# Eight modulation columns held to program order on VectorE, in a one-core encoder layer

## The chip, the cores and the metric

The kernel runs on one core of a Trainium2 chip. The metric is the device time of one execution in microseconds, lower is better; the median of several runs is compared. The core has five engines that work side by side, each with a queue of its own that it takes in order: TensorE (PE) for matmuls, VectorE (DVE), ScalarE (ACT), GpSimd (POOL) and SyncE (SP), which here only issues DMAs.

## The reference

One encoder layer on 512 tokens of width 1024, in float32, with nine modulation vectors computed from a conditioning vector `c`:

```python
c_act = jax.nn.silu(c)
mod = c_act @ w_mod + b_mod                 # 9 vectors of 1024
(sh1, sc1, g1, sh2, sc2, g2, sh3, sc3, g3) = jnp.split(mod, 9, axis=-1)

h = modulate(rmsnorm(x, norm_ffn1), sh1, sc1)
x = x + 0.5 * g1 * swiglu(h, w_ffn1_in, w_ffn1_out)

h = modulate(rmsnorm(x, norm_mix), sh2, sc2)
qa, ka, va, qb, kb, vb, ga, gb = jnp.split(h @ w_in, SPLIT_POINTS, axis=-1)
ya = window_gqa_sink(rope(qa), rope(ka), va, sink) @ w_branch_a   # 8 heads, |i-j| <= 128
yb = diff_attention(rope(qb), rope(kb), vb, lam) @ w_branch_b     # 4 heads, each normalised
x = x + g2 * ((sigmoid(ga) * ya + sigmoid(gb) * yb) @ w_out)

h = modulate(rmsnorm(x, norm_ffn2), sh3, sc3)
x = x + 0.5 * g3 * swiglu(h, w_ffn2_in, w_ffn2_out)
```

## The kernel before

Activations lie transposed, features on the 128 partitions and the 512 tokens along the free dimension, so `x` is eight tiles of 128 x 512. Every float32 product is made of three matmuls of a high and a low part (`mm3`); `split_from` makes the parts: ScalarE casts the high one (L179), VectorE subtracts for the low one (L180). The core does one stage after another: first feed-forward, shared projections, differential attention beside the gates, window attention beside the last gates and the two branches, output product, second feed-forward.

**The modulation columns.** Each of the nine vectors is stored as eight columns of 128 values. `mod_col(v, c)` computes one: VectorE multiplies a 128 x 1024 tile of `w_mod` with the conditioning row, copied to all partitions, and sums along the row (L266, one instruction). The tile is loaded by `mod_load` (L237) on SP's queue, 512 KB. The first two vectors are made at the start; the other 56 columns are spread over the layer in three lists: `rest` (G1, SC2, SH2) beside the first feed-forward, `later` (G2, SC3, SH3) beside the projections, and `latest`, the eight of G3, beside the gates that are left when the differential attention has ended (L1517). `column(columns)` takes the next column of a list, issues its load and puts it on `asked`; when more than `COLUMNS[...]` are asked for (2 for `later` and `latest`), the oldest is summed. So the sum of a column is traced two loads behind its own load. `beside` calls `column` after every fourth step of a gate; the `while` behind it (L1518) sums what is left. G3 is used only where the second feed-forward's product is added to `x` (L1625).

**What sets the order.** The Python program is traced once, which gives every instruction a place in the program's order. In this part of the layer (L1501 to L1539) the order of window attention, gates and branches in the program comes from `Line`, a planner by hand with costs and due times. Then the scheduler of the framework orders each engine's queue: by its own cost model it takes the instruction that is ready, and of several the first in the program. Inside `manual_schedule` blocks the order of the named engines is the program's; the stretch of this change is in none. So an instruction whose inputs the scheduler takes for ready early can go far ahead of its place. `tc.keep_in_program_order(ins)` adds one edge, without a wait: `ins` may not be queued ahead of the one instruction that was traced just before it on its engine. What is traced after it is free to go ahead of it.

In the program G3's columns stand so: column 0 is traced directly behind the two small VectorE instructions that `mod_begin` makes on the first use of G3 (L256, they read only `par`), which follow the third of four `turn_queries_a`; column 1 behind the fourth; column 2 behind `window_scores` of the second unit (its last VectorE instruction is L1420); column 3 behind two `window_turn` splits; columns 4 and 5 behind the scores of the third and fourth unit; columns 6 and 7 behind the split of the first window block's output.

**Buffers.** The loads of G3's columns take tiles of the `u4` ring, which has six. The window attention's `mask`, the reloaded conditioning row (`cact[0]`) and the transposed probabilities of `window_turn` come from the same ring.

Neighbours that the steps below name: `diff_norm` normalises a head of the differential attention (L1250 transposes, L1258 sums of squares on ScalarE, L1259 to L1261 on VectorE, L1262 a power on GpSimd, L1263 and L1264 on VectorE), and `diff_end` transposes the result again (`turned`, L1111) and splits it (L1275, L1276). `start_a` reads the window queries and values back from DRAM (L1345 to L1348), `turn_queries_a` transposes them (L1111) and splits them. `then_a` (L1523) and `then_b` (L1531, L1533) take the branches' results.

Of the kernel before, what the change touches and what calls it, by code (L numbers as in the profile page):

```python
# [128 lines left out]
def layer(ctx: ExitStack, tc: tile.TileContext, a: dict):  # L129
# [104 lines left out]
    def mod_load(v, c, w=None):  # L234
        if w is None:
            w = u4(F32).rearrange("p a b -> p (a b)")
        nc.sync.dma_start(w, a["w_mod"][v * NC + c])  # L237
        return w
# [4 lines left out]
    def mod_begin(v):  # L243
        if v in (SH1, SH2, SH3):
            return par[:, BMOD + v * NC : BMOD + (v + 1) * NC]
        if v not in begins:
            n = len(begins) * NC
            t = begins[v] = begin[:, n : n + NC]
            b = par[:, BMOD + v * NC : BMOD + (v + 1) * NC]
            if v in norms:  # L250
                V.scalar_tensor_tensor(t, b, 1.0, par[:, norms[v] : norms[v] + NC], ALU.add, ALU.mult)
            elif v == G3:

                t, b = (u.rearrange("p (n j) -> p n j", n=2) for u in (t, b))
                for j, by in ((slice(0, 2), -0.5), (slice(2, 4), 0.5)):
                    V.tensor_scalar(t[:, :, j], b[:, :, j], by, None, ALU.mult)  # L256
            else:
                V.tensor_scalar(t, b, 0.5, None, ALU.mult)
        return begins[v]

    def mod_col(v, c, w=None, in_order=False):
        if w is None:
            w = mod_load(v, c)
        t, b = modv[v][:, c : c + 1], mod_begin(v)[:, c : c + 1]
        by = 1.0 if v in norms or v in (SH1, SH2, SH3) else -0.5 if v == G3 and c % 4 < 2 else 0.5
        ins = V.tensor_tensor_reduce(  # L266
            out=w, in0=w, in1=cact[0], scale=by, scalar=0.0 if v in norms else b, op0=ALU.mult, op1=ALU.add,
            accum_out=t,
        )
        if in_order:  # L270
            tc.keep_in_program_order(ins)
        if v in norms:
            V.scalar_tensor_tensor(t, t, par[:, norms[v] + c : norms[v] + c + 1], b, ALU.mult, ALU.add)
# [168 lines left out]
    class Unit:  # L442
# [13 lines left out]
        asked, length = ("s1", "a11", "a12", "a22"), 1.0  # L456
# [229 lines left out]
    rest = [(v, c) for v in (G1, SC2, SH2, G2, SC3, SH3, G3) for c in range(NC)]  # L686
    rest, later, latest = rest[: EARLY * NC], rest[EARLY * NC : (EARLY + NEXT) * NC], rest[(EARLY + NEXT) * NC :]
# [59 lines left out]
    class Out1:  # L747
# [38 lines left out]
        def after(self, m):  # L786
            while any((v, c) == (G1, m) for v, c, *_ in rest + asked):
                column(rest)
            V.scalar_tensor_tensor(x[m], self.bank[m], modv[G1][:, m : m + 1], x[m], ALU.mult, ALU.add)
            if self.final:  # L790
                n2.add(m)
                spill(m)
# [6 lines left out]
    credit, asked = [0.0], []  # L799
# [4 lines left out]
    def column(columns):  # L804

        if columns:
            v, c = columns.pop(0)
            asked.append((v, c, mod_load(v, c, room[len(columns) % 2] if columns is rest else None)))
        if asked and (len(asked) > COLUMNS[columns is rest] or not columns):
            mod_col(*asked.pop(0), in_order=columns is rest)  # L810

    def side1(n=SIDE):

        while small_loads and len(rest) < 20:
            nc.sync.dma_start(*small_loads.pop())
        credit[0] += n
        while (rest or asked) and credit[0] >= 1.0:
            credit[0] -= 1.0
            column(rest)

    with tc.manual_schedule(engines={mybir.EngineType.SP, mybir.EngineType.Pool}):
# [62 lines left out]
        while rest or asked:  # L884
            column(rest)
# [751 lines left out]
    class Plain(Unit):  # L1637
        asked, more = ("a11", "a12", "a21", "a22"), {}
# [261 lines left out]
```

## Time and profile before

| | us |
|---|---|
| median of 3 runs | 1076.38 |
| lowest, highest | 1075.57, 1079.63 |
| profiled execution, its own time | 1076.98 |
| its span, first to last instruction | 1075.2 |
| TensorE busy | 1050.4 |
| VectorE busy | 797.0 |
| ScalarE busy | 568.0 |
| GpSimd busy | 154.0 |

TensorE's granted clock is 0.999 in the mean. In rows of the timeline the columns are start, duration, engine, source line, operation, output<-inputs, shape, count, and in brackets the engine's idle time before it and what ended it; `SPq` is a queue's issue of a DMA. In rows of waits they are who waited, for whom, the sum in us, how often, and the longest. In rows of DMA issues the last number is the median time from issue to landing. In rows of groups they are count, busy time and mean ns, and idle time before.

### The profile page before, as it was taken

The page shows a single profiled execution, that of the slowest core. Times are in us where ns is not written, and L with a number is a line of the kernel's source. Part 1 is how long each engine was busy: PE and PEld are TensorE (multiplying, and loading weights), DVE is VectorE, ACT ScalarE, POOL GpSimd, SP SyncE. Part 2 cuts the span into 40 slices and gives each one's busy share as a digit, 9 for nine tenths or more (in the row PEclk, how much of TensorE's full clock was granted, in tenths as well). Part 3 has the DMA queues.
Part 4 walks back from the last instruction along what each step waited for, and adds up shares of the span by engine and source line. Part 5 has one row for each costly group of instructions (what it writes and reads, how often), then busy time and mean ns, then how long its engine had stood idle before and what let it go on. Part 6 is the DMA issues. An engine that isn't in the chain of part 4 may idle for free. (4 is left out here: it accounts for less than half of the span.)

```text
span 1075.2 us, 18690 instructions
## 1 busy us (share of the span) xinstructions
PE 1050.4 (98%) x7316; PEld 955.6 (89%) x7316; DVE 797.0 (74%) x1459; ACT 568.0 (53%) x928; POOL 154.0 (14%) x174
## 2 busy tenths in 40 slices
PE   8999999999999999999998999999899999999998
PEld 6689889899998988898777888989889999999998
DVE  6985667576796679858774688945779777877877
ACT  5564335244354442657775666524766546664553
POOL 1100010100110100442211101001011111211210
PEclk9999999999999999999999999999999999999999
DMA  9968788866885369696368943843398899998974
GB/s 327 361 212 198 208 213 250 213 177 183 255 201 160 130 234 411 209 252 166 84 159 255 262 165 107 291 120 83 94 244 193 211 234 234 201 229 202 216 151 123
DMA packets 69083, 220.92 MB, mean 205 GB/s; under 512 B 8193, under 2 KB 10881, under 8 KB 68994
## 3 DMA queue, kind: packets, MB, share of 16 engines
q1 hardware_dynamic: 46512, 146.52, 38.3%
q0 software_dynamic: 19488, 68.70, 34.7%
q10 hardware_dynamic: 2994, 4.51, 1.1%
q8 instruction: 57, 0.93, 0.3%
q14 instruction: 32, 0.26, 0.1%
HBM read 209.46 MB, written 10.23 MB: 204 GB/s over the span
## 5 line engine op out<-in xcount | busy, mean ns | idle before, releaser
L179 ACT CAST high<-raw 128x1024 fp32r<-128x1024 f32 (+2 forms) x162 | 159.1, 986 | 190.1 <-PE sc L169 43.6
L180 DVE TENSOR_TENSOR low<-raw,high 128x1024 fp32r<-128x1024 f32 (+2 forms) x162 | 184.2, 1141 | 62.2 <-ACT high L179 60.4
L438 PE MATMUL acc<-b,high 128*128 128x256 f32 x508 | 141.0, 278 | 0.8 <-ACT f L512 0.7
L439 PE MATMUL acc<-b,high 128*128 128x256 f32 x508 | 140.7, 277 | 0.2 <-DVE b L1695 0.2
L440 PE MATMUL acc<-b,low 128*128 128x256 f32 x508 | 140.5, 277 | 0.0
L438 PE MATMUL sc<-b,high 128*128 128x256 f32 x500 | 138.6, 277 | 0.3 <-DVE f L514 0.3
L440 PE MATMUL sc<-b,low 128*128 128x256 f32 x500 | 138.5, 277 | 0.0
L439 PE MATMUL sc<-b,high 128*128 128x256 f32 x500 | 138.5, 277 | 0.0
L179 ACT CAST high<-u 128x1024 fp32r<-128x1024 f32 (+1 forms) x74 | 76.6, 1034 | 89.3 <-PE sc L169 30.3
L180 DVE TENSOR_TENSOR low<-u,high 128x1024 fp32r<-128x1024 f32 (+1 forms) x74 | 88.9, 1201 | 30.9 <-ACT high L179 29.2
L168 PE MATMUL sc<-b,high 128*128 128x512 f32 (+1 forms) x280 | 101.2, 361 | 0.6 <-ACT b L179 0.6
L169 PE MATMUL sc<-b,high 128*128 128x512 f32 (+1 forms) x280 | 100.7, 360 | 0.2 <-DVE b L180 0.2
L170 PE MATMUL sc<-b,low 128*128 128x512 f32 (+1 forms) x280 | 100.5, 359 | 0.0
L438 PEld LDWEIGHTS acc<-b,high 128*128 128x128 f32 x508 | 95.4, 188 | 1.3 <-ACT f L512 0.9
L439 PEld LDWEIGHTS acc<-b,high 128*128 128x128 f32 x508 | 95.5, 188 | 0.5 <-DVE b L1695 0.4
L440 PEld LDWEIGHTS acc<-b,low 128*128 128x128 f32 x508 | 95.3, 188 | 0.1
L438 PEld LDWEIGHTS sc<-b,high 128*128 128x128 f32 x500 | 94.1, 188 | 0.7 <-DVE f L514 0.5
L440 PEld LDWEIGHTS sc<-b,low 128*128 128x128 f32 x500 | 93.9, 188 | 0.1
L439 PEld LDWEIGHTS sc<-b,high 128*128 128x128 f32 x500 | 93.9, 188 | 0.0
L168 PE MATMUL acc<-b,high 128*128 128x512 f32 (+1 forms) x248 | 92.8, 374 | 0.0
L170 PE MATMUL acc<-b,low 128*128 128x512 f32 (+1 forms) x248 | 90.2, 364 | 0.0
L169 PE MATMUL acc<-b,high 128*128 128x512 f32 (+1 forms) x248 | 90.1, 363 | 0.0
(368 smaller groups left out, 2678.1 us busy)
## 6 DMA issues: line engine op xcount, KB each, us to landing
u<-w_mod SPq DMA_DIRECT2D x48, 512.0 KB, 7.5
raw<-w2i SPq DMA_DIRECT2D x31, 512.0 KB, 4.8
u<-w2i POOLq DMA_DIRECT2D x31, 512.0 KB, 6.6
b<-w_mod SPq DMA_DIRECT2D x24, 512.0 KB, 5.9
u<-w1u POOLq DMA_DIRECT2D x24, 512.0 KB, 7.5
raw<-w1u SPq DMA_DIRECT2D x24, 512.0 KB, 6.2
raw<-w1o SPq DMA_DIRECT2D x24, 384.0 KB, 4.0
raw<-w_gate SPq DMA_DIRECT2D x16, 512.0 KB, 7.3
```

The lines of the kernel that those rows point to most:

```text
L168: PE.matmul(out, wh, xh, start=first, stop=False)
L169: PE.matmul(out, wh, xl, start=False, stop=False)
L170: PE.matmul(out, wl, xh, start=False, stop=last)
L179: S.copy(hi, src)
L180: V.tensor_tensor(lo, src, f(hi), ALU.subtract)
L438: PE.matmul(out, wh[:, s], xh, start=first and j == 0, stop=False, skip_group_check=True)
L439: PE.matmul(out, wh[:, s], xl, start=False, stop=False, skip_group_check=True)
L440: PE.matmul(out, wl[:, s], xh, start=False, stop=last and j == 1, skip_group_check=True)
```

## The change

One argument changes. Before, `column` holds a column to the program's order only if it belongs to `rest`; after, it does so for all lists but `later`, so that the eight columns of `latest` are held as well. Loads, sums and their places in the program are the same.

```diff
         if asked and (len(asked) > COLUMNS[columns is rest] or not columns):
-            mod_col(*asked.pop(0), in_order=columns is rest)
+            mod_col(*asked.pop(0), in_order=columns is not later)
```

In `mod_col` this reaches:

```python
        ins = V.tensor_tensor_reduce(...)
        if in_order:
            tc.keep_in_program_order(ins)
```

## The prediction

> **What bounds the kernel now.** I read the page first (busy shares), then the busy time by stretch around the place of the change, then TensorE's waits, then the timeline of that place. A difference under 0.5% (5.4 us) is about what a measurement of this kernel can tell from no change.
>
> ```profile
> PE 1050.4 (98%) x7316; PEld 955.6 (89%) x7316; DVE 797.0 (74%) x1459; ACT 568.0 (53%) x928; POOL 154.0 (14%) x174
> 560.00:600.00 40.00, 36.96 (x203) 29.84 (x202) 21.72 (x61) 23.44 (x53) 6.50 (x7) 1.00 0.87 266
> 600.00:630.00 30.00, 29.80 (x174) 23.96 (x173) 22.15 (x74) 21.68 (x53) 1.73 (x2) 1.00 0.83 247
> 630.00:700.00 70.00, 70.00 (x487) 62.29 (x486) 61.38 (x160) 38.15 (x82) 4.30 (x8) 1.00 0.52 174
> 700.00:780.00 80.00, 76.11 (x518) 69.35 (x518) 49.17 (x83) 40.68 (x68) 5.84 (x7) 1.00 0.39 97
> PE tp L1111 <- DVE x L1264: 2.4, 1, 2.4
> ```
>
> In the rows by stretch the columns after the stretch are its length and the busy time of TensorE, its weight loads, VectorE, ScalarE and GpSimd, then the granted clock, the share of the DMA engines and GB/s. TensorE is the bound: 24.8 us of the span are not matmul time. The eight columns (L266, vector G3) run between 577 and 628 us. Around them TensorE is idle for 3.0 us in 560 to 600 and 0.2 us in 600 to 630, and 2.4 of these are one wait, for L1264. Nothing near the change can give back more than about 3 us, 0.3%. The gain is bounded tightly; a loss is not.
>
> **What the change removes: the columns that stand ahead of the last head's normalisation.** All eight columns cost the same before and after (1.28 us each, below); the change adds and removes no work, only places.
>
> ```profile
> L266 DVE CUSTOM_DVE_ANT_0 u<-u,u,begin 128x1024 f32<-128x1024 f32 x8 | 10.3, 1282 | 5.6 <-DMA u<-w_mod 5.6
> 577.43 1.29 DVE L266 CUSTOM_DVE_ANT_0 u<-u,u,begin 128x1024 f32<-128x1024 f32 x1 [3.07 <-DMA u<-w_mod]
> 577.56 0.22 ACT L1258 ACTIVATION_READ_ACCUMULATOR x<-op 128x1 f32 x1
> 578.64 0.16 DVE L1259 TENSOR_TENSOR sm<-sm 128x4 f32<-128x4 f32 x1
> 578.72 1.28 DVE L266 CUSTOM_DVE_ANT_0 u<-u,u,begin 128x1024 f32<-128x1024 f32 x1
> 579.92 0.16 DVE L1260 TENSOR_TENSOR sm<-sm,sm 128x4 f32<-128x4 f32 x1
> 580.12 0.17 DVE L1261 TENSOR_SCALAR sm<-sm 128x4 f32<-128x4 f32 x1
> 580.46 1.04 POOL L1262 TENSOR_TENSOR sm<-sm,half 128x4 f32<-128x4 f32 x1 [4.76 <-DVE sm L1261]
> 581.56 1.28 DVE L266 CUSTOM_DVE_ANT_0 u<-u,u,begin 128x1024 f32<-128x1024 f32 x1 [1.27 <-DMA u<-w_mod]
> 582.77 0.15 DVE L1263 TENSOR_TENSOR sm<-sm,sm 128x4 f32<-128x4 f32 x1
> 582.96 0.69 DVE L1264 TENSOR_TENSOR x<-op,sm 128x512 f32<-128x512 f32 x1
> 583.80 0.63 PE L1111 MATMUL tp<-ident,x 128*128 128x128 f32 x4 [2.45 <-DVE x L1264]
> 587.42 0.75 DVE L1276 SCALAR_TENSOR_TENSOR b<-tp,sub,b 128x512 fp32r<-128x512 f32 x1
> ```
>
> The normalisation's sums of squares are ready at 577.78 (ScalarE's last L1258). Then a small chain, L1259 to L1264, has to reach TensorE's transpose. Column 0 stands before L1259, column 1 before L1260, column 2 (waiting 1.27 us for its own load) before L1263; columns 3 and 4 stand before L1276. In the program all five are traced far behind this place: column 0 after the third window-query turn, the others later still.
>
> Column 0 stays where it is. Its pin ties it to the VectorE instruction traced just before it, and that is the second of the two small instructions of L256 that `mod_begin` emits on the first column of G3. These have floated to the very start of the run, and the change does not hold them:
>
> ```profile
> L256 DVE TENSOR_SCALAR begin<-par x2: 160/160/160, 7.8 to 9.8; 128x4 f32<-128x4 f32 x2
> ```
>
> Columns 1 to 7 are tied to window-attention instructions or to a held column and do move. Without columns 1 and 2 the chain goes: L1259 at 578.64, L1260 at 578.84, L1261 at 579.04, L1262 from 579.4 to 580.4, L1263 at 580.5, L1264 from 580.7 to 581.4, the transpose 0.15 us later at 581.5 (steps from the rows above: 0.2 us between small ones, 0.34 to GpSimd, 1.04 there). The transpose waited 2.45 us before 583.80, so TensorE was ready at 581.35. The stall shrinks from 2.45 to about 0.15: **-2.3 us** at this place (bounds: 0, if the scheduler puts something else there, and -2.45).
>
> **What is late next.** TensorE takes its matmuls in order, and 9.4 us further on stands the first transpose of the window queries, read back from DRAM.
>
> ```profile
> 582.73 0.46 SPq L1345 DMA_DIRECT2D f<-qa_scr  x1
> f<-qa_scr SPq DMA_DIRECT2D x1, 256.0 KB, 9.5
> 592.95 0.71 ACT L179 CAST b<-f 128x256 fp32r<-128x256 f32 x2 [2.08 <-DMA f<-va_scr]
> 593.16 0.60 PE L1111 MATMUL tp<-ident,f 128*128 128x128 f32 x4
> 570.00:600.00 30.00, 27.55 (x151) 22.75 (x151) 13.77 (x35) 15.56 (x31) 4.57 (x5) 1.00 1.02 313
> ```
>
> The first read was issued at 582.73 and took 9.5 us, so it landed at 592.2; va_scr, behind it in the same queue, only just made ScalarE's cast at 592.95. Before the change TensorE came at 593.16 and found the data. 2.3 us earlier it comes at 590.9 and waits 1.4. The read won't land earlier: the DMA engines are full here (share 1.02), the five w_mod loads ahead of it are issued as before (the first four take the free u4 slots, the fifth takes column 0's, which still ends at 578.7), and the SP queue reaches it only after two raw loads that pace on ScalarE. So of -2.3 us, **-0.9 us** is left, if the order on TensorE stays. [...]
>
> **What it adds: columns in the window attention's stretch.** The timeline shows where each predecessor ends, hence where columns 1 to 7 go.
>
> ```profile
> 603.09 0.68 DVE L180 TENSOR_TENSOR b<-tp,b 128x512 fp32r<-128x512 f32 x1
> 606.60 0.17 DVE L1420 TENSOR_SCALAR sm<-sm 128x4 f32<-128x4 f32 x1
> 609.35 0.17 DVE L1429 TENSOR_TENSOR sm<-sm,sm 128x4 f32<-128x4 f32 x1 [2.58 <-ACT x L1423]
> 610.63 0.68 DVE L180 TENSOR_TENSOR u<-acc,u 128x512 fp32r<-128x512 f32 x1
> 613.14 1.28 DVE L266 CUSTOM_DVE_ANT_0 u<-u,u,begin 128x1024 f32<-128x1024 f32 x1
> 615.30 1.28 DVE L266 CUSTOM_DVE_ANT_0 u<-u,u,begin 128x1024 f32<-128x1024 f32 x1
> 617.10 0.17 DVE L1420 TENSOR_SCALAR sm<-sm 128x4 f32<-128x4 f32 x1
> 619.76 0.56 DVE L1405 CUSTOM_DVE_ANT_0 x<-sc,u 128x384 f32<-128x384 f32 x1 [2.50 <-PE sc L176]
> 625.62 0.16 DVE L1420 TENSOR_SCALAR sm<-sm 128x4 f32<-128x4 f32 x1
> 626.35 1.28 DVE L266 CUSTOM_DVE_ANT_0 u<-u,u,begin 128x1024 f32<-128x1024 f32 x1
> 627.56 0.68 DVE L1523 SCALAR_TENSOR_TENSOR b<-f,acc 128x512 f32<-128x512 f32 x1
> ```
>
> Column 1 follows the fourth query split (603.8), in a busy place: +1.28 us on the first window chain. Column 2 follows the L1420 at 606.60 and falls into 2.58 us of idle. Column 3 follows the split at 610.63, again busy: +1.28. Against these, columns 5 and 6 leave 613.14 and 615.30: -2.56. Column 4 follows the L1420 at 617.10, into 2.50 us of idle. To here the chain is even. Column 5 then follows the L1420 at 625.62, and columns 6 and 7 a split near it: column 7 was there already, so the stretch 625 to 629 gets 2 x 1.28 = 2.6 us more, ahead of L1523, which empties a bank that TensorE needs again.
>
> On TensorE I take this at 0, bounds 0 and +2.6. What covers it is other matmuls, gates and then the first branch (70.00 of 70.00 us busy from 630 to 700), and the date on which the window attention is due:
>
> ```profile
> 675.28 0.68 DVE L180 TENSOR_TENSOR b<-op,b 128x512 fp32r<-128x512 f32 x1
> 622.52 0.29 PE L168 MATMUL op<-u,b 128*128 128x256 f32 x1
> 684.40 0.41 DVE L1531 SCALAR_TENSOR_TENSOR f<-f,acc 128x256 f32<-128x256 f32 x1
> u<-w_mod SPq DMA_DIRECT2D x3, 512.0 KB, 6.9
> ```
>
> Its last block is ready at 676.0. The second half of the last branch, which needs it, has its first result (the ninth L1531 of 16) at 684.40, and its matmuls begin some 2 us before (an estimate): about 6 us of cover.
>
> The loads of columns 5 to 7 move too. The u4 ring has six slots; the mask and the conditioning row hold two, held columns up to four, and the window attention's tiles take the others. So column 5's load waits for column 3 or a window tile (about 612.5); columns 5 and 6 still land by about 621, ahead of 625.6. Column 7's load goes when a tile of the second window unit comes free, after the `op<-u` products at 622.52, and at 6.9 us lands near 629.5, where its turn is at about 629: up to 1 us of wait, inside the bound above. Behind these loads in SP's queue are reads of the gates; nothing of the columns is on GpSimd's queue. G3 itself is read only by the last product, hundreds of us later.
>
> **Sum.** The profiled execution took 1076.98 us (span 1075.2 and 1.8 around it). -2.3 + 1.4 + 0 = -0.9 gives 1076.1. That execution is 0.6 above the median of the runs (1076.38), so I forecast **1075.5 us**; bounds of these terms alone 1073.9 and 1079 (nothing gained and 2.6 lost).
>
> **Rivals.** The whole stall comes back: TensorE's order or the landing shifts so that no wait replaces it: 1076.4 - 2.3 = 1074.1. For it: the second read-back has slack. Against: the 9.5 us row. [...]
>
> The change doesn't do what it says: column 0 certainly floats on; if the others' places in the queue come out as they are, 1076.4. Against: their predecessors wait for data that exists only after 603.
>
> Slower: held columns and window tiles share one ring, and VectorE waits at the head of its queue. If columns 5, 6 and 7 get slots one after another, each waits most of a 6.9 us load with the window chain behind it: about 14 us for two such waits, less 6 us of cover, gives +8: 1084. It decides once VectorE's waits for w_mod from 603 on pass 6 us; I count 1. The 3.07 us before 577.43 is such a wait in this trace. [...]
>
> Faster by over 0.5%: needs the 2.3 and, from a new order on TensorE, most of the 3.9 us idle between 700 and 780: 1076.4 - 6 = 1070.4. Nothing of the change reaches there.
>
> **Chances.** Forecast 0.45, whole stall 0.15, no effect 0.10 (all within 0.5%: 0.70); slower 0.20; faster 0.10. The range 1071.5 to 1081.5 holds the first three with their bounds, and the near edges of the two others.
>
> **What would show it.** Right: column 0 at about 577 and the other seven after 603; L1264 ending near 581.4; TensorE's wait on L1264 gone and one of about 1.4 us at the first `tp<-ident,f`. Wrong: columns 1 to 4 still before 590; no wait there; waits of L266 on w_mod after 603 over 6 us in sum; TensorE under 69 of 70 us between 630 and 700.

## The result and the profile after

| | before | after |
|---|---|---|
| median | 1078.14 us (22 runs) | 1081.77 us (22 runs) |
| profiled execution, its own time | 1076.98 us | 1083.54 us |
| its span | 1075.2 us | 1081.8 us |

The runs of both on one chip give a ratio of 1.0030, 95% interval 1.0018 to 1.0043: the change makes the kernel 0.3% slower, 3.6 us in the medians. The forecast was 1075.5 us, 0.9 below the time before.

TensorE's waits of the kernel after, in the row that takes the place of `PE tp L1111 <- DVE x L1264: 2.4, 1, 2.4`:

```profile
PE tp L1111 <- DMA f<-qa_scr: 4.5, 1, 4.5
```

The wait for L1264 is gone, and one of 4.5 us stands at the first window query. Busy time by stretch of the kernel after, the four stretches of the prediction and then the place of the wait (the columns behind the busy times are the granted clock, the share of the DMA engines, GB/s):

```profile
560.00:600.00 40.00, 34.89 (x184) 28.33 (x181) 13.79 (x41) 20.85 (x45) 6.51 (x7) 0.96 0.85 256
600.00:630.00 30.00, 29.90 (x174) 23.86 (x173) 24.54 (x81) 20.53 (x50) 1.73 (x2) 1.00 0.76 206
630.00:700.00 70.00, 69.04 (x482) 60.70 (x481) 62.45 (x164) 38.91 (x84) 4.33 (x8) 1.00 0.56 192
700.00:780.00 80.00, 77.25 (x516) 70.01 (x514) 49.02 (x84) 38.34 (x66) 4.98 (x6) 1.00 0.39 100
590.00:595.00 5.00, 1.56 (x7) 1.40 (x8) 0.00 (x0) 0.05 (x1) 0.00 (x0) 0.88 1.07 308
595.00:600.00 5.00, 5.00 (x28) 3.92 (x27) 2.71 (x10) 4.01 (x7) 0.87 (x1) 0.78 0.48 148
```

From 590 to 595 TensorE is busy for 1.56 us of 5, and the clock falls behind it: 0.88 and 0.78, that is 0.12 x 5 + 0.22 x 5 = 1.7 us of clock. From 630 to 700, where the kernel before had no idle time, there is 1 us. The timeline of the kernel after, VectorE first, then the reads and what was issued beside them:

```profile
575.28 1.28 DVE L266 CUSTOM_DVE_ANT_0 u<-u,u,begin 128x1024 f32<-128x1024 f32 x1 [2.63 <-DMA u<-w_mod]
578.36 0.16 DVE L1263 TENSOR_TENSOR sm<-sm,sm 128x4 f32<-128x4 f32 x1 [1.25 <-POOL sm L1262]
578.56 0.69 DVE L1264 TENSOR_TENSOR x<-op,sm 128x512 f32<-128x512 f32 x1
605.56 1.27 DVE L266 CUSTOM_DVE_ANT_0 u<-u,u,begin 128x1024 f32<-128x1024 f32 x1
...
629.89 1.28 DVE L266 CUSTOM_DVE_ANT_0 u<-u,u,begin 128x1024 f32<-128x1024 f32 x1
581.00 0.39 SPq L1345 DMA_DIRECT2D f<-qa_scr  x1
586.77 0.88 POOL L972 DMA_DIRECT2D low<-w_yb  x1 [5.00 <-ACT low L971]
593.44 0.73 PE L1111 MATMUL tp<-ident,f 128*128 128x128 f32 x4 [4.52 <-DMA f<-qa_scr]
```

Column 0 is where it was, and the other seven lie between 605.56 and 629.89; the chain L1259 to L1264 runs without a column in it. All that came as forecast. The read of the first window query, issued at 581.00, is waited for until 593.44.

**How much of it is in the place of the change.** The two profiles can be laid against each other by the same two matmuls of TensorE, one ahead of the change and one behind it. Kernel before, then kernel after:

```profile
569.09 0.66 PE L1111 MATMUL tp<-ident,x 128*128 128x128 f32 x4 [0.57 <-DVE u L180]
669.61 0.60 PE L1111 MATMUL acc<-ident,x 128*128 128x128 f32 x4
```

```profile
567.37 0.66 PE L1111 MATMUL tp<-ident,x 128*128 128x128 f32 x4 [0.56 <-DVE u L180]
673.27 0.60 PE L1111 MATMUL acc<-ident,x 128*128 128x128 f32 x4
```

100.5 us before (669.61 less 569.09), 105.9 after: 5.4 us more for the same matmuls. Ahead of this stretch the profiled kernel after is 1.7 us shorter than the one before, and behind it 2.9 us longer (408.5 against 405.6), with 3.4 us of clock lost near 780 and 795 us (below). In a second profile of the kernel after the part behind is 405.7 us, so that did not come again.

### The profile page after: what moved, and what is told of

Same layout as the page of the kernel before. It is cut to its first block, busy times and chain, and to the rows that moved or that the text cites. A ratio compares the mean times of both kernels' runs of the same rounds, so it can differ in the third digit from the quotient of the medians.

```text
span 1081.8 us, 18692 instructions
## 1 busy us (share of the span) xinstructions
PE 1054.0 (97%) x7316; PEld 958.3 (89%) x7316; DVE 798.0 (74%) x1459; ACT 567.9 (52%) x928; POOL 155.1 (14%) x174
## 5 line engine op out<-in xcount | busy, mean ns | idle before, releaser
L179 ACT CAST high<-raw 128x1024 fp32r<-128x1024 f32 (+2 forms) x162 | 159.1, 986 | 191.5 <-PE sc L169 44.2
L179 ACT CAST high<-u 128x1024 fp32r<-128x1024 f32 (+1 forms) x74 | 76.6, 1035 | 95.3 <-PE sc L169 31.8
L170 PE MATMUL sc<-b,low 128*128 128x512 f32 (+1 forms) x280 | 100.5, 359 | 0.0
```

Source lines behind the costliest of these rows:

```text
L170: PE.matmul(out, wl, xh, start=False, stop=last)
L179: S.copy(hi, src)
```

## The experiments

Theory A at the start: the front did it. Without the stall TensorE and ScalarE run 2.3 us earlier, so GpSimd's accumulate load of the first `w_yb` tile (512 KB) goes out earlier, into the stretch where the DMA engines are full (a share of 1.05 from 585 to 590 us in the kernel after), and the window queries' reads land later. Theory B: the back did it, by the columns' new places on VectorE. Theory C: neither, but a clock or an order that falls by chance. The table collects what the profiles of all runs say of the stretch between those two matmuls. "Waits at the reads" are TensorE's waits for `f<-qa_scr`; a figure behind a plus is its next wait, for the split of the value read `va_scr`. "Window products" are the 116 matmuls `sc<-ka,b`, `acc<-ka,b` and `acc<-ident,x`, each from its start to the next start, added up, with the waits that come right behind them. "Clock" is the time lost below a granted clock of 1.00 in 560 to 600. In kernels with added lines L1111 is L1112 or L1113, and L1264 and L1420 likewise.

| kernel | stretch | wait for L1264 | waits at the reads | window products | clock |
|---|---|---|---|---|---|
| before, two profiles | 100.5, 103.1 | 2.4, 3.8 | none | 12.5, 12.5 | 0, 1.7 |
| after, two profiles | 105.9, 105.3 | none | 4.5, 3.4 + 1.8 | 14.1, 14.1 | 1.7, 0 |
| columns 1 to 4 held, two | 102.3, 103.6 | none, 0.7 | 2.9, 3.2 | 12.5, 12.5 | 0, 0 |
| columns 5 to 7 held | 103.1 | 3.4 | none | 13.0 | 1.7 |
| after, the columns' loads held | 106.9 | 0.4 | 3.8 | 14.1 | 3.3 |
| after, `w_yb` by VectorE, two | 102.6, 104.8 | 0.8, 0.3 | 1.2 + 0.4, 2.8 | 14.1, 14.1 | 0, 1.7 |
| 1 to 4 held, `w_yb` by VectorE | 103.1 | 0.3 | 2.0 | 12.5 | 1.7 |
| 1 to 4 held, no accumulate load | 99.9 | 0.6 | none | 12.5 | 0 |
| before, no accumulate load | 100.4 | 2.3 | none | 12.5 | 0 |
| after, with filler matmuls | 106.7 | 0.7 | none | 14.6 | 0 |

**Front or back.** Two kernels hold one half of the columns each.

```diff
-            mod_col(*asked.pop(0), in_order=columns is not later)
+            v, c, w = asked.pop(0)
+            mod_col(v, c, w, in_order=columns is rest or (columns is latest and c < 5))
```

> Columns 1 to 4 are held to the program's order, columns 5 to 7 float as in the kernel before. Theory A (the loss is made at the front: without the wait for L1264 TensorE and ScalarE run 2.3 us earlier, GpSimd's 512 KB accumulate load low<-w_yb starts that much earlier inside the stretch of full DMA engines, the window queries' read f<-qa_scr takes some 12 us instead of 9.5, and TensorE waits 4 to 5 us at the first tp<-ident,f, its granted clock falling behind it): everything of the change's loss is here, ratio 1.002 to 1.004 to the kernel before, with the wait of 4 to 5 us for f<-qa_scr in the trace. Theory B (the loss is made at the back: held columns stand ahead of the window attention's own VectorE work from 603 to 631 us): columns 5 to 7, the ones that crowd 625 to 631, are free again, so ratio 0.999 to 1.001. Theory C (no place of its own; another draw of the scheduler's order): any value, and no wait of over 4 us at the read-back.

Measured: 1078.93 us, ratio 1.0013, interval 1.0000 to 1.0026; run a second time 1078.86, ratio 1.0007, 0.9988 to 1.0026. With `c >= 5` in place of `c < 5`:

> Columns 5 to 7 are held to the program's order, columns 1 to 4 float as in the kernel before, so columns 1 and 2 stand among the last head's normalisation again. Theory A: TensorE's wait of about 2.4 us for L1264 is back, the wait for f<-qa_scr at the first tp<-ident,f is under 1 us, the granted clock stays at 1.00 between 590 and 600 us, and the time is that of the kernel before: ratio 0.999 to 1.001. Theory B: the late columns alone cost what the change cost: ratio 1.002 to 1.004.

Measured: 1078.91, ratio 1.0016, 0.9998 to 1.0034. Both intervals overlap that of the whole change (1.0018 to 1.0043), so these times do not divide the loss; the profiles do. The first kernel's profile has waits at the reads, 2.9 us in two pieces (theory A expected 4 to 5 us in one), and the second has the wait for L1264 again, 3.4 us:

```profile
PE tp L1112 <- DMA f<-qa_scr: 2.9, 2, 1.6
```

```profile
PE tp L1112 <- DVE x L1265: 3.4, 1, 3.4
```

What separates the first from the full change is TensorE's queue. As built, TensorE's instructions stand in exactly the same order in the kernel before and in the one with columns 1 to 4 held; in the kernel after, the rows that differ all lie behind 621 us, in the window attention and the first branch beside it. Up to there the two kernels keep one distance. Kernel before, then kernel after:

```profile
603.85 0.73 PE L176 MATMUL sc<-ka,b 64*128 64x256 f32 x7
619.92 0.34 PE L176 MATMUL sc<-ka,b 64*128 64x384 f32 x1
```

```profile
605.72 0.73 PE L176 MATMUL sc<-ka,b 64*128 64x256 f32 x7
621.79 0.34 PE L176 MATMUL sc<-ka,b 64*128 64x384 f32 x1
631.83 0.50 PE L168 MATMUL acc<-b,high 128*128 128x512 f32 x1 [0.29 <-DVE b L1523]
652.55 0.38 PE L168 MATMUL op<-u,b 128*128 128x256 f32 x1 [0.66 <-ACT u L179]
```

Both are 1.87 us apart at the first and at the last, so in the kernel after columns 1 to 4 between 605 and 620 cost TensorE nothing: of theory B that part falls for it. Behind it the other order meets two waits, 0.29 and 0.66 us, that the kernel before does not have, and it divides the score products otherwise: two groups of 5 become one of 1 and one of 9, two of 6 become one of 8 and one of 4. Over the window products it comes to 14.1 us instead of 12.5, the same in every profile with that order, 12.5 in every profile with the order of before: **+1.6 us**, of which 1.0 are the two waits. Columns 5 and 6 make it: as built, the order of before comes with column 7 held beside 1 to 4, and the order of after with 1 to 6 held (read off the queues; these two kernels were not timed). With 5 to 7 held alone, and with the filler matmuls below, the order is another again, 13.0 and 14.6 us.

Where columns 1 to 4 are held alone, VectorE does cost TensorE something that the window products do not hold. From the first profile of that kernel:

```profile
616.99 1.28 DVE L266 CUSTOM_DVE_ANT_0 u<-u,u,begin 128x1024 f32<-128x1024 f32 x1 [0.28 <-DMA u<-w_mod]
618.20 0.16 DVE L1421 TENSOR_SCALAR sm<-sm 128x4 f32<-128x4 f32 x1
618.40 0.71 ACT L1424 ACTIVATE b<-b,sm,rqa 128x384 f32<-128x384 f32 x1 [1.45 <-DVE sm L1421]
621.79 0.38 PE L168 MATMUL op<-u,b 128*128 128x256 f32 x1 [0.69 <-ACT u L179]
```

One of the floating columns now stands ahead of the third unit's last small instruction (column 4 may not go ahead of that), ScalarE waits 1.45 us for it, and TensorE in turn 0.69 us for ScalarE's cast. All four profiles with 1 to 4 held and 5 to 7 free have this wait, 0.7 to 0.9 us, and another of 0.34 behind it; with no column held there is only one of 0.2. So theory B holds there with 0.8 to 1.0 us. The kernel after has no such wait at that place.

**The reads.** Two kernels were to take load off the DMA engines. The first holds the columns' loads:

```diff
-        nc.sync.dma_start(w, a["w_mod"][v * NC + c])
+        ins = nc.sync.dma_start(w, a["w_mod"][v * NC + c])
+        if v == G3:
+            tc.keep_in_program_order(ins)
```

> The changed kernel, and the eight columns' loads u<-w_mod are held to the program's order in SP's queue as well, so that the five that were issued at 570 us (2.5 MB in the stretch where the DMA engines are full) go after the reads of the window queries. Theory A: the reads f<-qa_scr find free DMA engines and land 2 us or more sooner after their issue; the wait at the first tp<-ident,f is under 1.5 us, the wait for L1264 stays away, the clock stays at 1.00: 2 to 3 us below the kernel before, ratio 0.997 to 0.999 (unless the later loads make VectorE wait for w_mod between 603 and 631 us by more than 6 us). Theory B: the columns' places on VectorE are unchanged, so ratio 1.002 to 1.004 as for the changed kernel, or more, by the later loads.

Measured: 1079.70, ratio 1.0023, 1.0007 to 1.0039. It says nothing on its question: five loads were still issued from 570.67 on. An edge ties a load only to the one traced just before it, and what stood there had gone ahead as well (argued from the edge's rule, not tried further).

```profile
570.67 7.85 SPq L237 DMA_DIRECT2D u<-w_mod  x5
588.34 0.88 POOL L974 DMA_DIRECT2D low<-w_yb  x1 [5.55 <-ACT low L973]
```

It served as one more profile of the loss: wait at the read 3.8 us, TensorE's queue as in the kernel after. The second takes the accumulate load away:

```diff
-            wh, wl = load(w[u])
+            wh, wl = (load_split if u == 0 else load)(w[u])
```

> The changed kernel, and the first tile of w_yb gets its low part from a subtraction on VectorE (one more L180 of 128x1024) instead of the accumulate load low<-w_yb on GpSimd's queue: one transfer of 512 KB less beside the reads of the window queries. Theory A: the read f<-qa_scr takes 9 to 10 us instead of 12.3, the wait at the first tp<-ident,f is 1 to 2.5 us instead of 4.5, the granted clock between 590 and 600 us stays near 1.00, and the time falls by 2.5 to 4 us below the changed kernel's: ratio to the kernel before 0.999 to 1.001. Theory B: nothing of this touches the back of the window stretch, ratio 1.002 to 1.004 as for the changed kernel. The subtraction itself takes about 1.3 us of VectorE.

Measured: 1079.53, ratio 1.0007, 0.9985 to 1.0028. It was run again with the second expectation:

> Columns 1 to 7 held and the first w_yb tile's low part by VectorE, a second time, for a second profile: the changed kernel's order on TensorE, no accumulate load among the reads. Theory A with both terms: the wait for f<-qa_scr is 1 to 2 us, the window attention's products and transposes take 14.1 us instead of 12.5; ratio 1.000 to 1.002, between the kernel with columns 1 to 4 held and this subtraction (1.000) and the changed kernel (1.003).

Measured: 1079.74, ratio 1.0016, 0.9998 to 1.0034. Taken together, the four reads of `qa_scr` land as they did before the change. DMA issues in 560 to 600, first the kernel before, then after, then this one (first run), the last number the median to landing:

```profile
f<-qa_scr SPq DMA_DIRECT2D x4, 256.0 KB, 8.7
```

```profile
f<-qa_scr SPq DMA_DIRECT2D x4, 256.0 KB, 11.5
```

```profile
f<-qa_scr SPq DMA_DIRECT2D x4, 256.0 KB, 8.6
```

and TensorE's wait in this kernel:

```profile
PE tp L1111 <- DMA f<-qa_scr: 1.2, 1, 1.2
```

In all kernels with the gates' accumulate loads in place that number is 8.3 to 8.7 where the one of `w_yb` goes out behind the reads or not at all, and 10.6 to 11.5 where it goes out among them (586.77 to 589.42 us); the last of the four lands 12.1 to 13.8 us after the first is issued in the one case, 14.9 to 16.3 in the other. So a load on GpSimd's queue slows reads that were issued ahead of it on SP's: in the kernel after it goes out 5.8 us behind the first of them (586.77 against 581.00), and their median is 11.5 us, against 8.3 and 8.6 in the two profiles of that kernel without it.

The first read alone, for which TensorE waits first, is not divided so clearly. In the kernel after:

```profile
f<-qa_scr SPq DMA_DIRECT2D x1, 256.0 KB, 12.3
```

It takes 9.5 to 12.3 us with the load among the reads and 9.5 to 11.1 without, and what else sets it stays open. In every profile with such a wait its first piece is, to within 0.4 us, the forecast 1.4 us plus what this read took beyond 9.5, less what was still waited at L1264. So the wait that stays without the load, 1.2 and 2.8 us, goes with reads of 9.9 and 11.1 us.

**The same kernels again, and the clock.**

> The kernel before itself, for a second profile and for what two equal kernels differ by here. Every theory: ratio 1.000 within its interval. TensorE's wait for L1264 of 2.4 us again, none for f<-qa_scr over 1 us; the granted clock falls in other places than in the first profile, if it falls by chance after the short waits near 780 and 790 us.

Measured: 1078.30 against 1078.60, ratio 1.0000, 0.9983 to 1.0016. The wait for L1264 was 3.8 us this time, and the clock lost 1.7 us behind it.

> The changed kernel itself, a second profile. Theory A, now with two terms that every execution has (the wait of 4.5 us for f<-qa_scr in place of 2.45 for L1264: +2.1; TensorE's own order of the window attention's matmuls from 621 us on, which is a different one: +1.6) and a clock that falls by chance: the wait of 4 to 5 us and the 1.6 us in the window attention are there again, ratio 1.003 to 1.004, and the loss near 780 us (2.7 us in the first profile of the changed kernel) need not be. Theory C (the clock is the loss): the clock falls at 590 to 600 us and near 780 us again, as in the first profile.

Measured: 1081.17 against 1078.60, ratio 1.0030, 1.0010 to 1.0050. The waits at the reads came to 3.4 and 1.8 us, the window products to 14.1; the clock stayed at 1.00 there. So theory C falls as the cause: between 560 and 600 us both kernels lose 1.7 us of clock in one profile and none in the other, and the mean clock over all runs with one on record is 0.9965 before (111 runs) and 0.9963 after (34), some 0.2 us of 1080. The first profile of the kernel after also lost clock near 780 us, behind waits of 1.1 and 1.5 us (1.4 and 1.6 in the kernel before):

```profile
780.00:785.00 5.00, 4.16 (x20) 3.95 (x21) 4.93 (x6) 3.90 (x8) 2.53 (x4) 0.66 0.41 49
795.00:800.00 5.00, 5.00 (x32) 5.00 (x31) 5.00 (x7) 3.84 (x6) 0.00 (x0) 0.66 1.03 268
```

0.34 x 5 is 1.7 us each; between 770 and 800 the first profile of before has 1.00 throughout, and the second of after loses 1.7 us once. Whether idle time makes the clock fall was tried with matmuls in the wait:

```diff
+FILL = 24
...
+        if g == 0 and i == 0:
+            fill = bank("tp")[:, 0:P]
+            for _ in range(FILL):
+                tc.keep_in_program_order(PE.matmul(fill, ident, ident, start=True, stop=True))
```

> The changed kernel, and 24 matmuls that nobody reads (128x128, identity by identity) stand on TensorE directly ahead of the first transpose of the window queries, in the time in which it waits for f<-qa_scr. They take some 3 us (estimate from 0.60 to 0.63 us for four transposes of that size), so the idle time falls from 4.5 to 1.5 us and no later work is due earlier. If idle time is what lowers the granted clock: 1.00 between 590 and 600 us, the matmuls behind the transpose at 0.23 us instead of 0.43, and 0 to 1.7 us below the changed kernel, ratio to the kernel before 1.0015 to 1.0035. If the clock falls for another reason (the DMA engines' load): 0.8 there as before.

Measured: 1084.54 (6 runs), ratio 1.0054, 1.0033 to 1.0074. The estimate of their size was wrong: each became two, 48 in 5.5 us, and they ran beyond the landing.

```profile
590.88 5.52 PE L1371 MATMUL tp<-ident 128*128 128x128 f32 x48
```

```profile
590.00:595.00 5.00, 5.00 (x42) 4.84 (x41) 0.76 (x2) 0.71 (x2) 0.00 (x0) 1.00 1.06 344
595.00:600.00 5.00, 5.00 (x40) 4.29 (x40) 0.70 (x2) 2.58 (x5) 0.00 (x0) 1.00 0.63 204
```

The time is lost, but the clock held at 1.00 under a DMA share of 1.06. Full DMA engines did not lower it by themselves: the first profile of the kernel before has 1.00 at shares of 1.02 to 1.06 from 585 to 600 us. In the two profiles each of the kernels before and after, every fall between 560 and 800 us stands behind waits of TensorE, from 1.1 us (near 780 in the first of after) to 4.5 us. But the clock also held in other kernels with a wait, so this one profile does not show that the filler kept it up.

**Both terms away.** Columns 1 to 4 held and the first `w_yb` tile by VectorE (the two edits above together):

> Columns 1 to 4 held, 5 to 7 floating (TensorE's order is then that of the kernel before), and the low part of the first w_yb tile by VectorE instead of the accumulate load. Theory A, all terms: the wait for L1264 shrinks from 2.45 to about 0.5, the reads of the window queries land some 10 us after issue and TensorE waits 1 to 1.5 us for them, no cost by TensorE's order: 0 to 1 us below the kernel before, ratio 0.999 to 1.000, against 1.001 with columns 1 to 4 held alone. Theory B (columns in the window stretch cost VectorE's time): 1.001 to 1.002, since VectorE gets the subtraction (1.3 us) on top.

Measured: 1079.46 against 1078.60, ratio 1.0003, 0.9988 to 1.0018: neither a loss nor a gain is shown. The last pair takes the accumulate loads of the last two gate tiles away as well, with and without held columns:

```diff
-            wh, wl = load_main(a["w_gate"][j])
+            wh, wl = (load_split if j >= 14 else load_main)(a["w_gate"][j])
```

> Columns 1 to 4 held (TensorE's order as in the kernel before), and the last two w_gate tiles and the first w_yb tile get their low parts by VectorE: no accumulate load is left beside the reads of the window queries. Theory A: the four reads and va_scr, which took 12 to 13 us from the first issue to the last landing without the w_yb accumulate load and 15 to 16 with it, come 2 to 3 us earlier once more; TensorE waits under 0.7 us for f<-qa_scr and under 0.7 for L1264, so this one is 1 to 2 us below the kernel before, ratio 0.998 to 0.999. Theory B (VectorE's load decides): three subtractions of 1.3 us stand ahead of L1264 and of the query splits, ratio 1.000 to 1.002.

Measured: 1078.28 against 1078.09, ratio 1.0001, 0.9983 to 1.0019. In its profile the reads take 5.3 us and are not waited for, and the stretch is the shortest of all:

```profile
f<-qa_scr SPq DMA_DIRECT2D x4, 256.0 KB, 5.3
```

```profile
581.26 0.63 PE L1112 MATMUL tp<-ident,x 128*128 128x128 f32 x4 [0.56 <-DVE x L1265]
```

> The kernel before with the same three low parts by VectorE, no column held: what the accumulate loads are worth without the change. Theory A: TensorE's wait for L1264 (2.4 to 3.8 us) stays, the reads are not waited for with or without the accumulate loads, so ratio 0.999 to 1.001. If the accumulate loads cost TensorE by themselves: 0.997 to 0.999 here too, and then the columns have no part in what the other kernel gains.

Measured: 1076.97 against 1078.09, ratio 0.9997, 0.9981 to 1.0014; its stretch is 100.4 us, with the wait for L1264 of 2.3 us. So with both stalls gone the stretch is only 0.5 us below this one, though the wait for L1264 is 1.7 us shorter. What the held columns give back stands in 600 to 630 us, first the kernel with columns 1 to 4 held, then this one:

```profile
600.00:630.00 30.00, 28.84 (x168) 22.65 (x166) 27.49 (x84) 19.64 (x44) 1.74 (x2) 1.00 0.80 235
```

```profile
600.00:630.00 30.00, 29.80 (x175) 23.78 (x174) 22.51 (x75) 21.25 (x50) 1.75 (x2) 1.00 0.84 243
```

VectorE has 5 us more to do there, and TensorE idles 1 us more, in the two waits described above (0.8 us for L179 and 0.34 here). The gain of 1 to 2 us that was expected is not shown by the times, and none of these kernels is shown to beat the kernel before.

> Columns 1 to 4 held, a second time, for a second profile: TensorE's order as in the kernel before, the accumulate load among the reads. Theory A with both terms: waits for f<-qa_scr (and what hangs on the later reads) of 3 us or more in sum, 12.5 us for the window attention's products and transposes as in the kernel before; ratio 1.000 to 1.002.

Measured as told above: waits at the reads 3.2 us, window products 12.5.

**Taken together.** Less the clock, the stretch is 100.5 and 101.4 before (101.0 in the mean), 104.2 and 105.3 after (104.7): +3.8. With columns 1 to 4 held alone it is 102.3 and 103.6 (+2.0: reads delayed, order as before), with all held and the `w_yb` load away 102.6 and 103.1 (+1.9: order changed, reads not delayed), with neither 101.4 (+0.4). From this last each term adds about 1.5, and both 3.4. Profiles of one kernel differ by 0.5 to 1.3 us in this figure, so the two terms add up to the whole, but each is known to about 1 us only; and the kernels with columns 1 to 4 held alone have 0.8 to 1.0 us of their own in it, which the kernel after does not have. One more profile of the same order and delayed reads, that with the columns' loads held, gives 103.6 (+2.6). The whole-run ratios stand in the same order: 1.0010 and 1.0012 in the mean of two, 1.0030 for both terms, 1.0003 for neither; their intervals overlap, so it is the profiles that carry the sizes.

## Why the prediction was wrong

- **The stall of 2.45 us goes** (-2.3): right. The kernel after has no wait for L1264 in either profile. In the second profile of before it was 3.8 us, so more was removed than forecast, 3.1 in the mean of two.
- **"The read won't land earlier"**: right as said, and mis-used. It was taken as "it lands at the same time", which sized the new wait at +1.4. It landed later: issued 1.73 us earlier than before, it took 12.3 us instead of 9.5, and 11.1 in the second profile, where the value read took 13.3 instead of 9.7 and cost 1.8 us more. The waits were 4.5 and 5.1 us. This is the step that failed first. The prediction followed what stands ahead of the read in its own queue, and not what the earlier TensorE releases on another: ScalarE's L971 came earlier, and with it GpSimd's load, which had gone at 591.16, behind the reads, and now goes at 586.77 (1.7 us of this is that the whole stretch starts earlier in this profile). Without that load the wait was 1.2 and 2.8 us: near the 1.4 once, twice it the other time. How the 1.4 was reckoned from the read's length was right; the length was wrong.
- **The window stretch at 0 (bounds 0 and +2.6)**: +1.6, inside the bounds, but mostly from another cause: 0.3 us of it is the wait for L1523 that the prediction named, 0.7 a wait for ScalarE's L179, and the rest the new groups. The columns' places on VectorE came as derived, their times within about 1 us of the derived ones once the 1.87 us by which this stretch is late are taken off; no column waited for its load after 603, and columns 1 to 4 cost TensorE nothing up to 620 us. The step that failed is the condition "if the order on TensorE stays": columns 5 and 6 made the scheduler order the window products anew. It was named, for TensorE's gain only, and given no price.
- **Clock**: not in the sum. It does not separate the kernels, but adds 1.7 us to a single execution each time it falls (3.4 in two profiles), three times from 590 us on in the first profile of the kernel after.
- **Sum**: forecast -2.3 + 1.4 + 0 = -0.9. In the means of two profiles: -3.1 + 4.8 + 1.6 = +3.3, against +3.8 in the stretch and 3.6 and 2.6 us between the medians of the two comparisons. The 1075.5 also stood on a median of three runs, 1076.38, where 22 runs of the kernel before give 1078.14; that moves the forecast time, not its wrong sign.
- **The rivals**: the whole stall coming back (1074.1) needed a read that lands early; among the kernels with columns held only the one without accumulate loads had it (5.0 us). The slower rival had the right sign by a mechanism that did not occur: waits of L266 on `w_mod` after 603 were none, where it needed 6 us.

## What to carry to other kernels

When a stall is taken away, follow what the freed engines issue earlier, on every queue: a transfer that used to go out behind a read can now go out beside it, and here the late read cost TensorE more than the stall had (4.8 us against 3.1). An edge that holds one engine's instruction can change the order that a scheduler gives to another engine, and what stays free can float into the place that was cleared; compare the queues of all engines before a term is set to nothing. For effects under 0.5%, take a second profile of each kernel and compare stretches between the same two instructions, so that what falls by chance is seen as such.

## What the runs showed of the hardware

What a wait does to the clock differs from one execution to the next. After a wait it went to 0.50 for some 3.4 us (1.7 us of clock lost), for 6.8 us (3.4 us lost; behind 3.8 us of waiting with the columns' loads held, and behind 3.4 us near 788 with columns 1 to 4 held and no accumulate load), or not at all, and the length of the wait alone did not decide: 2.0 us of idle time lowered it in one kernel (columns 1 to 4 held, `w_yb` by VectorE; first group below, every second us), 3.4 us did not in the second profile of the kernel after (second group).

```profile
592.00:593.00 1.00, 0.04 (x1) 0.00 (x0) 0.00 (x0) 0.00 (x0) 0.00 (x0) 1.00 1.05 406
594.00:595.00 1.00, 0.94 (x6) 0.87 (x7) 0.01 (x1) 0.44 (x2) 0.00 (x0) 0.75 1.05 414
596.00:597.00 1.00, 1.00 (x4) 0.81 (x3) 0.47 (x1) 1.00 (x2) 0.00 (x0) 0.50 0.21 86
598.00:599.00 1.00, 1.00 (x10) 0.74 (x10) 0.00 (x0) 0.33 (x2) 0.55 (x1) 1.00 0.68 262
```

```profile
590.00:595.00 5.00, 1.65 (x8) 1.06 (x8) 0.00 (x0) 0.00 (x0) 0.30 (x1) 1.00 1.07 325
595.00:600.00 5.00, 3.21 (x17) 2.33 (x17) 1.45 (x3) 2.55 (x6) 0.00 (x0) 1.00 0.75 242
```

What else decides it is not shown by these runs.
